# Modulation terms on TensorE, another order of products in the first pass, and other banks, in a two-layer decoder trunk

## The chip, the cores and the metric

The kernel runs on one NeuronCore of a Trainium2 chip. The metric is device time in microseconds of one execution, as the median of several runs. An engine here is one of TensorE (PE; its weight loads are shown apart as PEld), VectorE (DVE), ScalarE (ACT), GpSimd (POOL) and SyncE (SP, which here only issues transfers). Each has its own queue, and works it off in order.

## The reference

Two layers over 256 tokens of width 1024, in float32. Each layer mixes tokens and then runs a gated feed-forward network with a short convolution. Layer 0 mixes by attention in three dilated groups of 16 heads of 64, whose results share one softmax; layer 1 by gated linear attention. Each sub-layer is normalised and then shifted and scaled by terms that come from a vector `c`:

```python
mod = jax.nn.silu(c) @ w_ada[i] + b_ada[i]          # 6 pieces of 1024 per layer
sh1, sc1, g1, sh2, sc2, g2 = [m[:, None, :] for m in jnp.split(mod, 6, axis=-1)]
h = rmsnorm(x, norm_mix[i]) * (1.0 + sc1) + sh1
y = dilated_mixture(h, w_in_a[j], w_out_a[j], rel_bias)   # layer 0
x = x + g1 * y
h = rmsnorm(x, norm_ffn[i]) * (1.0 + sc2) + sh2
x = x + g2 * conv_ffn(h, w_up[i], conv_w[i], conv_b[i], w_down[i])
```

In the dilated mixture, `qkv = h @ w_in` gives queries, keys and values of the three groups; the scores get a bias by distance from `rel_bias`; probabilities times values give the output of a head.

## The kernel before

`x` lies transposed, 8 tiles (`KT`) of 128 features by 256 tokens (`T`). Every large product is made of three: an operand is split into a high part in the fast float32 format and a low part that is the remainder, and `mm3` (lines 172 to 177) issues high x high, high x low and low x high. For a weight matrix, `split` (line 155) loads it into a buffer `raw` (four in turn), ScalarE copies it into `whi` (line 165), VectorE subtracts to get `wlo` (line 169); three buffers of each. For the activations, `normed` (line 253) makes `xr = x * a * r` on VectorE (line 257), `hhi` on ScalarE (line 259) and `hlo` on VectorE (line 260).

The modulation terms come in 48 chunks of 2 x 128 terms (`ada_chunk`, line 129): the chunk's weights are loaded, VectorE makes a dot product over 1024 for each term (line 138) with `c_bc`, which is silu of `c` repeated on all partitions, and ScalarE adds bias and scale (lines 146 and 148). Chunk `kt` of layer 0 gives shift and scale of tile `kt`; the others are made further on, by `next_ada`, wherever the program calls it.

The opening: `c` is loaded as one row and spread by TensorE with `ones_d` (`cb`, line 123), ScalarE makes silu of it (line 124); x is squared, half on VectorE (line 357) and half on ScalarE (line 360); VectorE adds tiles of squares (line 363), TensorE sums over partitions (`ms`, line 187), and ScalarE makes the reciprocal root with Ln and Exp (`rstd_of`). `keep_warm` (line 266) puts matmuls of a constant on TensorE. Three small products give the rows of the biases (line 377), which go through a buffer in DRAM (`rows_d`).

The first pass (lines 381 to 395 and 563 to 572) does the work of head pairs 0 and 1 together: `w0` has, for each of the 8 tiles, 15 blocks of 128 columns: queries and keys of pair 0 in three groups, values of pair 0, queries and keys of pair 1. All accumulate in the 8 banks of PSUM, of 512 columns each. The banks are handed out in three rings: `p` of 2, `s` of 4, `t` of 2. Within a tile the products go block by block, three for each block.

Behind it come the pairs: `queries` (line 534) makes queries and keys of one group of a pair (48 matmuls), `evacuate` (line 488) copies them out, `values` (line 523) makes half of the values, `scores` (line 410) the scores in the four `s` banks, `probabilities` (line 428) adds the bias and takes maxima on VectorE (line 438), exponentials on ScalarE (line 447) and normalised probabilities, `turn` (line 457) transposes those on TensorE through a `t` bank and copies them out (line 464), alternating ScalarE and VectorE, and `outputs` (line 467) multiplies with the values. `load_bias` (line 337) reads a pair's biases with eight transfers. The written order after the first pass is: values of pair 1 (first half), scores of pair 0, values of pair 1 (second half), queries of pair 2, transposes and scores of pair 1, and from there a loop over pairs 2 to 7.

The order on each queue is settled when the program is built: a planner simulates the engines and lays each engine's instructions in a row, following data and `behind(...)`. `behind(i)` keeps what is issued inside it on the engine of `i` behind `i` in that row, and does not touch other engines. Every transfer of weights is issued on SP's queue, in turn with those of the bias rows; `c`, the small vectors and the table go through ScalarE's.

## Time and profile before

| | |
|---|---|
| median of 3 runs | 774.31 us (772.75 to 777.1) |
| profiled execution | 777.02 us, span of its instructions 775.1 us |
| instructions | 15908 |
| TensorE busy | 755.9 us, 98% (weight loads 731.5 us, 94%) |
| VectorE busy | 633.7 us, 82% |
| ScalarE busy | 484.7 us, 63% |
| GpSimd busy | 12.4 us, 2% |
| read from HBM | 184.17 MB, 239 GB/s over the span |
| mean granted clock of TensorE | 0.994 |

In a row of the timeline stand the start in us, the length in us, the engine, the line of the kernel, the operation, `out<-in`, the shapes and the count of instructions merged; in brackets the idle time before it and what ended it. In a row of waits stand who waited on which line, for whom, the total in us, how many times, and the longest. Rows of TensorE overlap, since its matmuls are pipelined: the distance between two starts is the cost of one. A float32 matmul is shown as two instructions.

### The profile page before, as it was taken

Reading aid. Unit: us, or ns where it says so; the run is one execution under the profiler, and the core shown is the slowest. Engines: PE = TensorE matmul, PEld = TensorE weight load, DVE = VectorE, ACT = ScalarE, POOL = GpSimd, SP = SyncE. Lnnn points to the kernel's source line nnn. Section 1 sums busy time; section 2 is a strip of 40 time slices with the busy share of each in tenths; the row PEclk is TensorE's granted clock in tenths of the full one; section 3 lists DMA queues with packets and bytes.
Section 4 is the critical chain, followed back from the end, with each engine's and each line's share of the span. In section 5 each row is a group of like instructions: output and inputs, shape, how many; then the busy total and the mean of one; then the engine's idle time right before and its main releaser. Section 6 shows DMA issues by size and latency. Waiting matters only on the chain.

```text
span 775.1 us, 15908 instructions
## 1 busy us (share of the span) xinstructions
PE 755.9 (98%) x6416; PEld 731.5 (94%) x6416; DVE 633.7 (82%) x1136; ACT 484.7 (63%) x948; POOL 12.4 (2%) x36
## 2 busy tenths in 40 slices
PE   8899899999999999999999999999999999999997
PEld 5899899999999999999999998898999999999997
DVE  6996787779879968999998877797667998899662
ACT  5566564655666668766666556746667776667552
POOL 0000000000000010000000100000010000000000
PEclk9999999999999999999999999999999999999999
DMA  8988687686887847767646985966245665555741
GB/s 344 413 296 315 186 315 242 231 327 198 319 313 257 296 163 261 272 224 270 209 160 213 353 297 180 344 243 235 95 166 188 219 218 187 194 199 205 252 161 55
DMA packets 36199, 186.29 MB, mean 240 GB/s; under 512 B 8412, under 2 KB 10972, under 8 KB 19870
## 3 DMA queue, kind: packets, MB, share of 16 engines
q1 hardware_dynamic: 35744, 184.84, 66.8%
q8 instruction: 50, 0.82, 0.4%
q10 hardware_dynamic: 382, 0.45, 0.2%
q14 instruction: 23, 0.19, 0.1%
HBM read 184.17 MB, written 1.10 MB: 239 GB/s over the span
## 4 chain that ended last, share of the span: by engine, by line
PE 71%; DMA 12%; DVE 11%; ACT 3%; issue 1%; SPq 0%; DVEq 0%; ACTq 0%
PE pab L176 10%; PE pab L175 10%; PE pab L177 10%; DMA raw<-in_wqk 8%; DVE wlo L169 5%; PE pd L175 5%; PE pd L177 5%; PE pd L176 5%; DMA raw<-in_wv 3%; PE pqk L175 3%; PE pqk L176 2%; DVE ada_raw L138 2%; PE pqk L177 2%; PE py L175 2%; PE py L176 2%; PE py L177 2%
## 5 line engine op out<-in xcount | busy, mean ns | idle before, releaser
L169 DVE TENSOR_TENSOR wlo<-raw,whi 128x1024 fp32r<-128x1024 f32 (+3 forms) x274 | 291.8, 1098 | 62.8 <-ACT whi L165 62.1
L165 ACT CAST whi<-raw 128x1024 fp32r<-128x1024 f32 (+3 forms) x274 | 245.8, 945 | 131.9 <-PE pab L176 41.3
L177 PE MATMUL pab<-hhi,wlo 128*128 128x256 f32 x672 | 184.9, 276 | 0.0
L176 PE MATMUL pab<-hlo,whi 128*128 128x256 f32 x672 | 184.8, 277 | 0.0
L175 PE MATMUL pab<-hhi,whi 128*128 128x256 f32 x672 | 183.4, 277 | 0.0
L176 PEld LDWEIGHTS pab<-hlo,whi 128*128 128x128 f32 x672 | 126.1, 188 | 0.2
L177 PEld LDWEIGHTS pab<-hhi,wlo 128*128 128x128 f32 x672 | 126.2, 188 | 0.0
L175 PEld LDWEIGHTS pab<-hhi,whi 128*128 128x128 f32 x672 | 125.2, 188 | 0.1
L175 PE MATMUL pqk<-hhi,whi 128*128 128x256 f32 x440 | 120.8, 286 | 2.6 <-ACT hhi L259 2.6
L177 PE MATMUL pqk<-hhi,wlo 128*128 128x256 f32 x440 | 121.7, 281 | 0.0
L176 PE MATMUL pqk<-hlo,whi 128*128 128x256 f32 x440 | 121.6, 280 | 0.0
L138 DVE CUSTOM_DVE_ANT_0 ada_raw<-ada_raw,c_bc 128x1024 f32<-128x1024 f32 x96 | 113.6, 1222 | 6.6 <-DMA ada_raw<-in_w_ada 6.6
L177 PE MATMUL pd<-ghi,wlo 128*128 128x256 f32 x352 | 97.1, 276 | 0.0
L176 PE MATMUL pd<-glo,whi 128*128 128x256 f32 x352 | 97.1, 276 | 0.0
L175 PE MATMUL pd<-ghi,whi 128*128 128x256 f32 x352 | 96.8, 276 | 0.0
L175 PEld LDWEIGHTS pqk<-hhi,whi 128*128 128x128 f32 x440 | 82.3, 191 | 3.8 <-ACT hhi L259 3.1
L177 PEld LDWEIGHTS pqk<-hhi,wlo 128*128 128x128 f32 x440 | 83.4, 190 | 0.3 <-issue 0.3
L176 PEld LDWEIGHTS pqk<-hlo,whi 128*128 128x128 f32 x440 | 83.5, 190 | 0.1
L176 PEld LDWEIGHTS pd<-glo,whi 128*128 128x128 f32 x352 | 66.1, 188 | 0.0
L177 PEld LDWEIGHTS pd<-ghi,wlo 128*128 128x128 f32 x352 | 66.1, 188 | 0.0
L175 PEld LDWEIGHTS pd<-ghi,whi 128*128 128x128 f32 x352 | 65.9, 188 | 0.0
L734 ACT ACTIVATE r<-pab,small 128x256 f32<-128x256 f32 x86 | 46.6, 558 | 15.6 <-DVE r L737 15.5
(210 smaller groups left out, 1266.4 us busy)
## 6 DMA issues: line engine op xcount, KB each, us to landing
ada_raw<-in_w_ada SPq DMA_DIRECT2D x47, 1024.0 KB, 5.8
raw<-in_w_up SPq DMA_DIRECT2D x42, 1024.0 KB, 4.9
raw<-in_w_down SPq DMA_DIRECT2D x32, 704.0 KB, 5.1
raw<-in_wqk SPq DMA_DIRECT2D x18, 1024.0 KB, 6.6
raw<-in_wv SPq DMA_DIRECT2D x14, 768.0 KB, 4.6
raw<-in_w SPq DMA_DIRECT2D x7, 960.0 KB, 6.5
raw<-in_w_out_a SPq DMA_DIRECT2D x4, 1024.0 KB, 7.2
raw<-in_w_v_b SPq DMA_DIRECT2D x4, 1024.0 KB, 6.4
```

Of the source, the lines that this page charges most:

```text
L138: nc.vector.tensor_tensor_reduce(w, w, c_bc, op0=ALU.mult, op1=ALU.add, scale=1.0, scalar=0.0, accum_out=dot,)
L165: copied[0] = nc.scalar.copy(hi[:, c], raw[:, c])
L169: last_lo[0] = nc.vector.tensor_tensor(lo[:, c], raw[:, c], hi[:, c].bitcast(F32), op=ALU.subtract)
L175: mm(ps, a[0], b[0], start=start, stop=False)
L176: mm(ps, a[0], b[1], start=False, stop=False)
L177: return mm(ps, a[1], b[0], start=False, stop=stop)
L734: nc.scalar.activation(r, u[:, :T], AF.Identity, scale=cw[2], bias=col(C_CB + 44 * l + f))
```

## The change

The opening makes the two terms of chunk (0, 0) on TensorE. Its weights are laid out anew on the host, as 16 blocks of 128 x 128. `c` is loaded a second time as columns (`c_col`, each column twice), with silu in `silu_c`; each block is the stationary operand of a matmul with two columns of `silu_c` moving, and the sums for shift and scale accumulate in one bank, from which ScalarE reads. The other chunks stay on VectorE. `keep_warm(4)` moves ahead of `cb`. Tiles 4 to 7 of the squares are no longer added on VectorE: the mean square takes five matmuls instead of two. `keep_warm(3)` and the rows of the biases go behind the new matmuls.

In the first pass, a tile's products go by part: first high x high for all 15 blocks, then `whi` with `hlo`, then `wlo` with `hhi`. The preparation is written out, with VectorE's order fixed: the tile's dots, `xr`, first half of `wlo`, `hlo`, second half; the next tile's dots behind that. For the first three tiles ScalarE's order is fixed too: the terms, half of the cast, `hhi`, the other half. The banks of pair 0 are `s`, `t`, `t`, its values in `p`, `p`; those of pair 1 `s`, `s`, `s`.

Behind the pass the copies out go groups 1, 2, 0 of pair 0 first, then pair 1. Then come, in this order, the queries and keys of group 0 of pair 2 (in a `t` bank), the scores of pair 0, both halves of the values of pair 1, the scores of pair 1, and the loop. `probabilities` is cut in two (`maxima` and the rest), and pair 1's second part and pair 0's outputs go into the loop's first turn. In `turn`, tiles 2 and 3 take banks of ring `s`, in all pairs.

```diff
--- before.py
+++ after.py
...
     c_row = wspl.tile([P, 2048], F32, tag="whi", name="c_row")
     nc.scalar.dma_start(c_row[:1, :D], I["c"])
+    c_col = const.tile([P, 2 * KT], F32, name="c_col")
+    nc.scalar.dma_start(c_col, I["c_col"])
...
+    def keep_warm(n):
+        ps = bank("warm")
+        for i in range(n):
+            mm(ps[:, :P], ones_d, ones_d, start=True, stop=True)
+    keep_warm(4)
+    silu_c = const.tile([P, 2 * KT], F32, name="silu_c")
+    nc.scalar.activation(silu_c, c_col, AF.Silu)
     c_bc = const.tile([P, D], F32, name="c_bc")
...
+        if (l, n) == (0, 0):
+            ps = bank("mod", "p")
+            for i in range(2 * KT):
+                last_mod[0] = mm(ps[:, 2 * (i % 2) : 2 * (i % 2) + 2], raw[:, P * i : P * i + P], silu_c[:, i // 2 * 2 : i // 2 * 2 + 2],
+                   start=(i == 0), stop=(i == 2 * KT - 1))
...
+            if (l, n) == (0, 0):
+                dot = ps[:, 2 * s : 2 * s + 1]
+            else:
...
-    for n in (0, 4):
-        for m in (2, 1):
-            last_add = nc.vector.tensor_tensor(sq[:, n : n + m, :], sq[:, n : n + m, :], sq[:, n + m : n + 2 * m, :], op=ALU.add)
-        if n == 0:
-            with behind(last_add):
-                last_add = scale_terms(0)
+    for m in (2, 1):
+        last_add = nc.vector.tensor_tensor(sq[:, 0:m, :], sq[:, 0:m, :], sq[:, m : 2 * m, :], op=ALU.add)
+    with behind(last_add):
+        scale_terms(0)
...
-    r = rstd_of([sq[:, 0, :], sq[:, 4, :]])
+    r = rstd_of([sq[:, i, :] for i in (0, 4, 5, 6, 7)])
+    with behind(norm_ops[1]):
+        term = ada_chunk(0, 0, dmas=2)
...
+    with behind(norm_ops[0], last_mod[0]):
...
+    n0 = 15 * P
+    halves0 = (slice(0, n0 // 2), slice(n0 // 2, n0))
+    before_dots, cast = (), ()
...
         if kt:
-            w0.append(split(I["w0"][kt], 15 * P))
-        else:
-            with behind(chain[0][1]):
-                w0.append(split(I["w0"][kt], 15 * P, 2, after=((term,), (chain[0][0],))))
-            with behind(copied[0]):
+            with behind(*before_dots):
+                term = ada_chunk(0, kt, dmas=2 if kt == 1 else 1)
+        a, sh = mod[0, 1, kt], mod[0, 0, kt]
+        xr = tmp.tile([P, T], F32, tag="xr", name="xr")
+        hhi, hlo = h_hi[kt][:, :], h_lo[kt][:, :]
+        last_dve = nc.vector.scalar_tensor_tensor(xr, x[kt], a[:, 0:1], r, op0=ALU.mult, op1=ALU.mult)
+        raw = wraw.tile([P, 2048], F32, tag="raw", name="raw")
+        for c in halves0 if kt < 2 else (slice(0, n0),):
+            last_load[0] = nc.sync.dma_start(raw[:, c], I["w0"][kt][:, c])
+        whi = wspl.tile([P, 2048], F32R, tag="whi", name="whi")
+        wlo = wspl.tile([P, 2048], F32R, tag="wlo", name="wlo")
+        with behind(*((term,) if kt < 3 else ()), *cast):
+            cast = nc.scalar.copy(whi[:, halves0[0]], raw[:, halves0[0]])
+        with behind(*((cast,) if kt < 3 else ())):
+            last_hhi = nc.scalar.activation(hhi, xr, AF.Identity, bias=sh[:, 0:1])
+        with behind(*((last_hhi,) if kt < 3 else ())):
+            cast = (nc.scalar.copy(whi[:, halves0[1]], raw[:, halves0[1]]),)
+        for i in range(3):
+            with behind(last_dve):
+                if i == 1:
+                    last_dve = nc.vector.scalar_tensor_tensor(hlo, xr, sh[:, 0:1], hhi.bitcast(F32), op0=ALU.add, op1=ALU.subtract)
+                    chain[kt] = chain[7] = last_hhi, last_dve
+                else:
+                    c = halves0[i // 2]
+                    last_dve = nc.vector.tensor_tensor(wlo[:, c], raw[:, c], whi[:, c].bitcast(F32), op=ALU.subtract)
+        before_dots = (last_dve,)
+        h.append((h_hi[kt], h_lo[kt]))
+        w0.append((whi, wlo))
+        if kt == 0:
+            with behind(*cast):
...
     def turn(tiles, normed_p, pt):
         for i in tiles:
-            t = bank("t", "t")
+            t = bank("t", "ttss"[i])
...
         if g:
-            last_q[0] = nc.scalar.mul(q[g], pq, 0.125)
-            return nc.vector.tensor_copy(k[g], pk)
+            i = nc.scalar.mul(q[g], pq, 0.125)
+            return i, nc.vector.tensor_copy(k[g], pk)
...
-        return nc.vector.tensor_tensor(kl, pk, kh.bitcast(F32), op=ALU.subtract)
+        nc.scalar.mul(qh, pq, 0.125)
+        i = nc.scalar.copy(kh, pk)
+        nc.vector.scalar_tensor_tensor(ql, pq, 0.125, qh.bitcast(F32), op0=ALU.mult, op1=ALU.subtract)
+        return i, nc.vector.tensor_tensor(kl, pk, kh.bitcast(F32), op=ALU.subtract)
...
-    def values(u, half, pv):
+    def values(u, half, pv, after=(), low=()):
         with behind(*chain[7]):
-            w = split(I["wv"][u - 1, half], 1536)
+            w = split(I["wv"][u - 1, half], 1536, after=(after, after), low=low, late=low)
...
-    def queries(u, g, q, k, tag="p", after=()):
-        w = split(I["wqk"][u - 2, g], 2048, after=(after, after))
+    def queries(u, g, *qk):
+        pq, pk, middle, end = raw_queries(u, g)
+        with behind(evacuate(*qk, g, pq, pk)[1]):
+            next_ada()
+        return middle, end
+    def raw_queries(u, g, tag="p", low=()):
+        w = split(I["wqk"][u - 2, g], 2048, low=low, late=low)
...
-    b0 = [bank("pqk", tg) for tg in "ssspp"]
+    b0 = [bank("pqk", tg) for tg in "sttpp"]
     pqk0 = [b[:, T * i : T * i + T] for b in b0[:3] for i in range(2)]
     pv = b0[3:]
-    b1 = [bank("pqk", tg) for tg in "stt"]
+    b1 = [bank("pqk", tg) for tg in "sss"]
...
     for kt in range(KT):
-        s, e = kt == 0, kt == KT - 1
-        for i in range(2 * NG):
-            mm3(pqk0[i], parts(w0[kt], P * i), h[kt], s and i % 2 == 0, e and i % 2 == 1)
-        wv = parts(w0[kt], 6 * P, NG * P)
-        for t in range(2):
-            ht = [y[:, P * t : P * t + P] for y in h[kt]]
-            mm3(pv[t][:, : NG * P], ht, wv, s, e)
-        for i in range(2 * NG):
-            mm3(pqk1[i], parts(w0[kt], 9 * P + P * i), h[kt], s and i % 2 == 0, e and i % 2 == 1)
+        whi, wlo = w0[kt]
+        hhi, hlo = h[kt]
+        for part, (w, y) in enumerate(((whi, hhi), (whi, hlo), (wlo, hhi))):
+            s, e = part == kt == 0, part == 2 and kt == KT - 1
+            for piece in range(3):
+                if piece == 1:
+                    for t in range(2):
+                        mm(pv[t][:, : NG * P], y[:, P * t : P * t + P], w[:, 6 * P : 9 * P], start=s, stop=e)
+                    continue
+                at, ps = ((0, pqk0), None, (9 * P, pqk1))[piece]
+                for i in ((2, 3, 4, 5, 0, 1), (), range(6))[piece]:
+                    mm(ps[i], w[:, at + P * i : at + P * i + P], y, start=s and i % 2 == 0, stop=e and i % 2 == 1)
...
-    v = by_groups(pv)
-    for qk, pqk, g in ((qk0, pqk0, 0), (qk1, pqk1, 0), (qk0, pqk0, 1), (qk0, pqk0, 2), (qk1, pqk1, 1), (qk1, pqk1, 2)):
-        evacuate(*qk, g, pqk[2 * g], pqk[2 * g + 1])
-    pv = [bank("pv", "p") for _ in range(2)]
-    end = values(1, 0, pv)
+    left = [evacuate(*qk, g, pqk[2 * g], pqk[2 * g + 1])
+            for qk, pqk, g in ((qk0, pqk0, 1), (qk0, pqk0, 2), (qk0, pqk0, 0), (qk1, pqk1, 0), (qk1, pqk1, 1), (qk1, pqk1, 2))]
+    pq, pk, middle, end = raw_queries(2, 0, tag="t", low=left[0][1:])
+    with behind(left[-1][0], left[-3][0]):
+        v0 = by_groups(pv)
     bias = bias_of(0)
     with behind(end):
         s, last = scores(*qk0)
+    qk = new_qk()
+    evacuated = evacuate(*qk, 0, pq, pk)
+    pv = [bank("pv", "p") for _ in range(2)]
     with behind(last):
-        values(1, 1, pv)
-    v0, v = v, by_groups(pv)
-    before = probabilities(s, bias)
-    qk = new_qk()
-    with behind(last):
-        end = queries(2, 0, *qk, tag="t", after=last_q)
-    bias = bias_of(1)
-    with behind(end[1]):
-        turn((0, 1), *before)
+        values(1, 0, pv, low=left[-1][1:])
+    end = values(1, 1, pv, after=left[-1][:1], low=evacuated[1:])
+    with behind(evacuated[1]):
+        next_ada()
+    v = by_groups(pv)
+    before = probabilities(*maxima(s, bias))
+    bias1 = bias_of(1)
+    with behind(end):
         s, last = scores(*qk1)
-    with behind(last):
-        turn((2, 3), *before)
-        outputs(0, v0, before[1])
-    before = probabilities(s, bias)
+    raised = maxima(s, bias1)
...
-            with behind(last):
+        with behind(last):
+            if u > 2:
                 queries(u, 0, *qk)
-        middle, end = queries(u, 1, *qk)
+            middle, end = queries(u, 1, *qk)
...
-        queries(u, 2, *qk)
+        if u == 2:
+            turned_pt, before = before[1], probabilities(*raised)
+        middle, end = queries(u, 2, *qk)
+        if u == 2:
+            with behind(end):
+                outputs(0, v0, turned_pt)
+                turn((0, 1), *before)
         pv = [bank("pv", "p") for _ in range(2)]
         end = values(u, 0, pv)
+        if u == 2:
+            with behind(end):
+                turned = turn((2, 3), *before)
...
     A["w_ada"] = wa.reshape(2, 24, 2, D, P).transpose(0, 1, 4, 2, 3).reshape(2, 24, P, 2 * D)
+    A["w_ada"][0, 0] = wa[0, :2].reshape(2, KT, P, P).transpose(2, 1, 0, 3).reshape(P, 2 * D)
+    A["c_col"] = np.repeat(vec(a["c"]), 2, axis=1)
...
```

38 lines of the change are left out of this document (12 added, 26 removed).

## The prediction

> **What bounds the kernel now.** I read the page first, then TensorE's waits, then the timeline of the first 100 us engine by engine, then busy time by windows.
>
> ```profile
> span 775.1 us, 15908 instructions
> ...
> PE 755.9 (98%) x6416; PEld 731.5 (94%) x6416; DVE 633.7 (82%) x1136; ACT 484.7 (63%) x948; POOL 12.4 (2%) x36
> ...
> PE t L463 <- ACT pt L464: 4.3, 4, 2.6
> ...
> PE pqk L175 <- ACT hhi L259: 2.6, 2, 2.2
> ...
> PE po L471 <- DVE pt L464: 0.9, 1, 0.9
> ...
> PE s L418 <- DVE k L501: 0.8, 1, 0.8
> ```
>
> TensorE is busy for 755.9 of 775.1 us, so no edit can win more than its idle time (19.2 us) plus the time in which it is busy at half clock. The change touches the part up to the attention pairs, where these waits lie. The other waits of the span sum to about 2 us. The reader should see three places.
>
> The first is the opening, up to the first product of the first pass at 13.72.
>
> ```profile
> 3.06 3.74 PE L123 MATMUL cb<-c_row,ones_d 1*128 1x512 f32 x4 [3.06 <-DMA c_row<-in_c]
> 6.74 2.07 PE L270 MATMUL warm<-ones_d 128*128 128x128 f32 x8
> 7.34 1.14 ACT L360 ACTIVATE sq<-x_all 128x512 f32<-128x512 f32 x2
> 8.61 2.33 PE L187 MATMUL ms<-sq,ones_d 128*128 128x256 f32 x4
> 9.58 1.22 DVE L138 CUSTOM_DVE_ANT_0 ada_raw<-ada_raw,c_bc 128x1024 f32<-128x1024 f32 x1
> 10.73 1.21 PE L270 MATMUL warm<-ones_d 128*128 128x128 f32 x6
> 11.80 0.28 ACT L148 ACTIVATE mod<-dot,small 128x1 f32<-128x1 f32 x1
> 11.99 0.38 ACT L146 ACTIVATE mod<-dot,one_b,small 128x1 f32<-128x1 f32 x1
> 12.28 0.97 ACT L165 CAST whi<-raw 128x960 fp32r<-128x960 f32 x1
> 12.41 0.48 DVE L257 SCALAR_TENSOR_TENSOR xr<-x_all,mod,rstd 128x256 f32<-128x256 f32 x1 [0.46 <-ACT mod L146]
> ```
>
> Call T the end of the second modulation term (11.99 + 0.38 = 12.37): all that follows hangs on it. The first product comes 1.35 later, behind one cast and one `hhi`.
>
> The second place is the first pass, eight tiles of x against `w0`.
>
> ```profile
> 13.72 0.50 PE L175 MATMUL pqk<-hhi,whi 128*128 128x256 f32 x2 [0.38 <-ACT hhi L259]
> 21.74 1.01 PE L175 MATMUL pqk<-hhi,whi 128*128 128x256 f32 x3 [2.25 <-ACT hhi L259]
> 49.81 0.34 PE L175 MATMUL pqk<-whi,hhi 128*128 128x384 f32 x1
> 55.02 0.34 PE L175 MATMUL pqk<-whi,hhi 128*128 128x384 f32 x1
> 59.87 0.34 PE L175 MATMUL pv<-whi,hhi 128*128 128x384 f32 x1
> ...
> 31.11 0.48 DVE L257 SCALAR_TENSOR_TENSOR xr<-x_all,mod,rstd 128x256 f32<-128x256 f32 x1
> 31.50 1.22 DVE L138 CUSTOM_DVE_ANT_0 ada_raw<-ada_raw,c_bc 128x1024 f32<-128x1024 f32 x1
> 33.79 0.48 DVE L260 SCALAR_TENSOR_TENSOR hlo<-xr,mod,hhi 128x256 fp32r<-128x256 f32 x1
> 36.33 0.48 DVE L257 SCALAR_TENSOR_TENSOR xr<-x_all,mod,rstd 128x256 f32<-128x256 f32 x1
> 50.21 2.23 DVE L169 TENSOR_TENSOR wlo<-raw,whi 128x960 fp32r<-128x960 f32 x2 [0.27 <-ACT whi L165]
> ```
>
> One tile costs TensorE 55.02 - 49.81 = 5.21 and VectorE 36.33 - 31.11 = 5.22, of which two dots are 2.29 (31.50 to 33.79) and `xr`, `hlo` and two halves of `wlo` 2.93. The two engines are matched. Eight tiles make 41.7 on TensorE, yet the pass takes 59.87 - 13.72 = 46.15. The 4.45 between are the stall of 2.25 at 21.74 and the half clock behind it:
>
> ```profile
> 4.60:8.00 3.40, 3.40 (x9) 1.59 (x8) 2.51 (x5) 1.75 (x4) 0.00 (x0) 1.00 0.99 344
> 8.00:11.40 3.40, 3.35 (x12) 2.45 (x12) 2.86 (x5) 2.18 (x3) 0.00 (x0) 1.00 1.03 396
> 18.20:21.60 3.40, 1.30 (x11) 1.09 (x10) 3.40 (x6) 1.71 (x4) 0.00 (x0) 1.00 1.01 417
> 21.60:25.05 3.45, 3.31 (x13) 3.31 (x14) 3.45 (x7) 2.46 (x5) 0.00 (x0) 0.52 1.01 415
> 79.66:83.07 3.41, 1.14 (x10) 0.93 (x8) 1.37 (x2) 2.42 (x4) 0.00 (x0) 1.00 0.34 55
> 83.07:86.50 3.43, 3.05 (x15) 3.06 (x16) 3.43 (x11) 0.69 (x2) 0.00 (x0) 0.52 0.85 356
> ```
>
> Columns: window, length, busy time of PE, PEld, DVE, ACT, POOL, granted clock, DMA share, GB/s. Twice a window in which TensorE worked for only 1.1 to 1.3 of 3.4 us is followed by one of the same length at clock 0.52. Each costs about 0.48 x 3.4 = 1.65 us over the stall itself.
>
> The third place is the stall at 80.8.
>
> ```profile
> 50.52 0.60 SPq L347 DMA_DIRECT2D bias<-rows_d  x1
> ...
> 66.86 0.63 SPq L159 DMA_DIRECT2D raw<-in_wqk  x1
> 80.62 1.99 ACT L165 CAST whi<-raw 128x1024 fp32r<-128x1024 f32 x2 [3.11 <-DMA raw<-in_wqk]
> 82.64 0.38 ACT L496 ACTIVATE q<-pqk 128x256 fp32r<-128x256 f32 x1
> 83.45 0.90 PE L463 MATMUL t<-ident,pn 128*128 128x128 f32 x3 [2.65 <-ACT pt L464]
> ```
>
> A transpose waits for a bank `t`. That bank is freed by copies on ScalarE, which stand behind casts of weights issued at 66.86 and landed at 80.62. Those weights are not what TensorE needs next: it is ScalarE's queue that is blocked.
>
> **The change, part by part.**
>
> *Opening.* The two dots of chunk (0, 0) leave VectorE (2.3 us from 9.58). TensorE gets 16 matmuls with the weight block stationary and 2 columns moving. A float32 matmul shows as two passes (four copies of the warm matmul make x8), so these are 32. The mean square goes from 2 matmuls to 5, that is from 4 passes to 10, for two pairs of VectorE adds saved. The nearest rows for the new matmul are the cold warm-up (8 passes from 6.74 to 8.61, 0.23 each) and this one, late in the run and with the same 2 columns:
>
> ```profile
> 766.93 0.50 PE L1043 MATMUL ms<-ones_d,sqacc 128*128 128x2 f32 x4
> ```
>
> That is 0.125 a pass. So 32 passes cost 4.0 warm and 7.4 cold. Ten passes of 256 columns cost 4.6 cold (half of a 512-column pass of the 3.06 row, 3.74 / 4 / 2 = 0.46) and 2.3 warm. TensorE is free of `cb` at about 7.0. The operands arrive from then on: the chunk was there by 9.58, the squares at 8.5. The windows put an edge of the clock at 11.4 (25.05 less four times 3.42), where the passes of the 10.73 row begin to cost less. I take the same edge: from 7.0 to 11.4, 4.4 of the 12.0 cold us are done, and the other 7.6 take 3.8, so the terms' sums end at 15.2. Warm throughout it would be 7.0 + 6.3 = 13.3, cold throughout 19.0. The two ScalarE terms take 0.6 more (11.80 to 12.37): T = 15.8, bounds 13.9 and 19.6, against 12.37. So the opening loses 3.4 (1.5 to 7.2). The idle 3.06 before `cb` covers the moved warm-up, whose removal behind `cb` frees nothing on the path. The extra DMA for `c_col` goes before `small`, `tab` and `oh` on ScalarE's queue, and what waits for those, needed only near T, has slack. Chunk (0, 0)'s buffer comes free at 15.2 instead of 11.9, so chunk 2 is asked for 3 us later; its dots come at about T + 9.7, over 10 us after that.
>
> The Trainium skill, TensorE: Matmul & The Clock Gate, section "Part 1: The HAM clock gate", says that the clock doubles once the array was busy through a window of about 3.4 us, whatever the matmuls. By that rule the moved warm-up and `cb`, busy from about 1.2, would run warm before 8. The trace speaks against it for matmuls with one row of weights: TensorE was busy all through 4.60 to 8.00, yet the passes from 8.00 to 11.40 were still at the cold price.
>
> *First pass in order of parts.* TensorE now needs `hlo` a third and `wlo` two thirds into a tile, so the stall of 2.25 goes. VectorE becomes what sets the pace: its order is fixed as dots, `xr`, half of `wlo`, `hlo`, other half, and the next tile's dots stand behind these. The dots no longer run a tile ahead, so each `xr` waits for the terms just made: 0.46, as in the 12.41 row. In the first three tiles the cast also stands behind the term, 0.97 against 0.4 for `xr`: 0.5 more. VectorE: 3.5 for tile 0 (2.93 + 0.5), two tiles of 5.22 + 0.46 + 0.5 = 6.2, five of 5.7; sum 44.4. After the last `wlo` half TensorE has a values piece and a pair piece left, 1.0. The pass ends at T + 45.4, where before it was 59.87 - 12.37 = 47.5: 2.1 won. TensorE's own bound, T + 1.35 + 41.7 and at most 1.65 for a cold start, T + 44.7, lies just under it. With the later T the pass ends 1.3 later than now. Transfers keep up, since the pace of 5.7 asks for less than now.
>
> *Third pair's first weights behind the pass.* VectorE ended its part of the pass at 52.44 (50.21 + 2.23), save one `xr` and `hlo`, 7 us ahead of TensorE, and had the next weights split. Now it ends 1.0 ahead, and must copy a key (0.41) and make half of a `wlo` of 1024 columns (2.36 for two) before the third product: about 0.6 of a new stall. In return the scores come behind 48 matmuls of 0.115 (5.5 us) in place of 24 of 0.17 (4.1), so that their wait of 0.8 goes. On SP's queue the pair's weights now go ahead of the first bias rows, and the loads of the values' weights behind them: eight issues of about 0.6, as in the 50.52 row, 4.8 us. The values are wanted only after the pair's 5.5 us and the scores, so this is hidden behind those; without that cover it would cost up to 4.8.
>
> *The order of pairs and the banks.* The queries of pair 2 leave their bank before the values and scores follow, so the transposes no longer need it at 80.8; tiles 2 and 3 use `s` banks. What is late next is the cast of the weights landed at 80.62, needed only with the second following query step, at about 84. I take the stall (2.65) and its half clock (1.65) as won: 4.3, bounds 0 and 4.3. The other three waits of transposes, 4.3 - 2.65 = 1.7, go too; bounds 0 and 1.7. The 0.9 of `po` I leave.
>
> **Sum.** +3.4 - 2.1 + 0.6 - 0.8 - 4.3 - 1.7 = -4.9. The profiled execution took 777.02 (span 775.1 and 1.9 around it), 2.7 above the median of the runs, 774.31. So 772.1 in such an execution, **769.4** by the median.
>
> **Rivals.**
>
> *TensorE is warm in the opening.* If the moved warm-up and `cb` count, the sums end at 13.3 and T is 13.9: 1.9 less than I took, 767.5. For it: TensorE is occupied from about 1.2. Against it: the two first windows above. (By the Trainium skill's rule on the clock, cited above, this would be the time.)
>
> *The stall moves, so that the gain of the banks is lost.* ScalarE's queue is still an order written before the run. If a cast stands ahead of an evacuation and its transfer is late, the wait and the half clock come back: 769.4 + 4.3 = 773.7. For it: large loads and bias rows still lie close together. Against it: the queue's loads are wanted later in TensorE's order.
>
> *Slower: casts ahead of the terms.* In the pass both casts of a tile may stand on ScalarE between the dot and the second term, as the existing queue does from tile 4 on:
>
> ```profile
> 32.97 1.88 ACT L165 CAST whi<-raw 128x960 fp32r<-128x960 f32 x2
> 34.75 0.38 ACT L146 ACTIVATE mod<-dot,one_b,small 128x1 f32<-128x1 f32 x1
> ```
>
> Today the term has until 36.33; afterwards VectorE, and through it TensorE, waits for it at once. At 1.88 for each of five tiles this is 9.4: 778.8. It makes the kernel slower by over 0.5% from about 1.8 a tile; one cast a tile (4.7) gives 774.1, no change. Against it: the term is ready before the second cast in most tiles.
>
> **Numbers.** Forecast 0.44 (own range 766.5 to 772.5), warm opening 0.24, moved stall 0.20, casts 0.12. A measurement of this kernel can tell about 0.5%, 3.9 us, from no change: faster ends at 770.4, slower begins at 778.2. Faster: the warm opening and about four fifths of the forecast, 0.59. Slower: most of the casts' case, 0.11. Within: 0.30. The range runs from 762 (no loss in the opening, 766.0; the new stall of 0.6 hidden and the 2 us of waits that I left gone, 763.4; a median as far down as the lowest run is now, 1.6) to 777 (one cast a tile, 774.1, and a median as far up as the highest run is now, 2.8).
>
> **What would show it.** Right: the first `xr` near 15.8; 32 passes into the bank of the terms at 0.23 first and 0.125 later; VectorE without a gap over 1 us in the pass and a tile in 5.7; no wait of 2 us for `hhi`; no wait for `t` near 80; clock 1.00 from 25 to 100. Wrong: T at or before 12.4 (then the time is about 766), a tile over 6.5 on VectorE, a wait over 2 us between the pass and the seventh step behind it, or a row of the later pairs with new waits for `s`.

## The result, and the profile after

The changed kernel takes 787.28 us as the median of 6 runs (782.56 to 791.98), beside 774.87 for the kernel before (772.75 to 777.1, 6 runs): a ratio of 1.0159, with an interval of 1.0118 to 1.0200. It is slower by 12.4 us. The forecast was 769.4, with a range that ended at 777. One sentence of the description above is wrong: `keep_warm(4)` does not move ahead of `cb`, a second call of it is added there, and the old one behind `cb` stays.

From the page of the changed kernel, span and busy times:

```profile
span 785.1 us, 16005 instructions
...
PE 767.0 (98%) x6462; PEld 740.4 (94%) x6462; DVE 630.1 (80%) x1130; ACT 484.9 (62%) x949; POOL 12.6 (2%) x36
```

Its waits of TensorE (who waited on which line, for whom, total, times, longest):

```profile
PE pqk L613 <- ACT hhi L409: 5.8, 5, 4.0
PE pv L194 <- DVE k L528: 2.4, 2, 2.0
PE pv L195 <- DVE wlo L188: 1.5, 3, 0.7
```

The waits of transposes for `pt` are gone. In their place stand a wait of the first pass for `hhi` and, late in the loop over the pairs, waits of values for a key copy (2.0 of the 2.4 at 260) and for `wlo`.

The timeline of its opening and first pass (TensorE, VectorE, ScalarE and one issue of SP):

```profile
6.91 2.08 PE L126 MATMUL warm<-ones_d 128*128 128x128 f32 x8
9.63 2.20 PE L148 MATMUL mod<-silu_c,ada_raw 128*128 128x2 f32 x16
11.69 1.97 PE L206 MATMUL ms<-sq,ones_d 128*128 128x256 f32 x8
13.50 1.84 PE L148 MATMUL mod<-silu_c,ada_raw 128*128 128x2 f32 x16
15.92 0.49 DVE L400 SCALAR_TENSOR_TENSOR xr<-x_all,mod,rstd 128x256 f32<-128x256 f32 x1 [7.27 <-ACT mod L165]
...
50.15 0.33 SPq L403 DMA_DIRECT2D raw<-in_w  x1
56.99 1.00 ACT L407 CAST whi<-raw 128x960 fp32r<-128x960 f32 x1 [3.11 <-DMA raw<-in_w]
58.79 0.29 ACT L167 ACTIVATE mod<-dot,small 128x1 f32<-128x1 f32 x1
60.06 1.99 ACT L184 CAST whi<-raw 128x1024 fp32r<-128x1024 f32 x2 [0.98 <-DMA raw<-in_wqk]
61.95 0.38 ACT L165 ACTIVATE mod<-dot,one_b,small 128x1 f32<-128x1 f32 x1
62.37 0.48 DVE L400 SCALAR_TENSOR_TENSOR xr<-x_all,mod,rstd 128x256 f32<-128x256 f32 x1 [4.21 <-ACT mod L165]
63.45 1.65 PE L613 MATMUL pqk<-hhi,whi 128*128 128x256 f32 x6 [3.96 <-ACT hhi L409]
71.04 0.28 PE L194 MATMUL pqk<-hhi,whi 128*128 128x256 f32 x1
71.76 0.38 PE L196 MATMUL pqk<-hhi,wlo 128*128 128x256 f32 x1 [0.32 <-DVE wlo L188]
```

In this execution T is 15.9, the forecast number. The last tile is what goes wrong. Its own casts wait 3.11 for a load that was asked for at 50.15. Its second term then stands on ScalarE behind the two casts of the third pair's first weights, which wait another 0.98 for their load and take 1.99. VectorE waits 4.21, TensorE 3.96, and a stretch at half clock follows (columns as in the windows shown before):

```profile
60.00:64.00 4.00, 0.55 (x2) 0.55 (x3) 1.63 (x3) 2.79 (x4) 0.00 (x0) 0.70 0.53 92
64.00:68.00 4.00, 4.00 (x20) 4.00 (x19) 1.39 (x2) 0.91 (x2) 0.00 (x0) 0.50 0.90 358
```

The first pass ends at 71.04 (the first `pqk` row of line 194) and not at 59.87. The first start of a product, before and after, by tile: `po` (outputs of the heads) 95.4 and 101.4, `py` (the projection behind all pairs) 260.8 and 269.8, `pab` (the feed-forward network) 291.3 and 300.0, `y` (the end) 767.3 and 777.5. So 11.2 are lost by the end of the pass, 5.2 are won back up to `po`, 3.0 of these are lost again in the loop over the pairs, and 10.2 stand at the end of the two profiled executions.

### The profile page after: what moved, and what is told of

It is laid out like the page before. It is cut to its first block, busy times and chain, and to the rows that moved or that the text cites. A ratio compares the mean times of both kernels' runs of the same rounds, so it can differ in the third digit from the quotient of the medians.

```text
span 785.1 us, 16005 instructions
## 1 busy us (share of the span) xinstructions
PE 767.0 (98%) x6462; PEld 740.4 (94%) x6462; DVE 630.1 (80%) x1130; ACT 484.9 (62%) x949; POOL 12.6 (2%) x36
## 4 chain that ended last, share of the span: by engine, by line
PE 67%; DMA 14%; DVE 13%; ACT 3%; issue 2%; SPq 1%; ACTq 0%; DVEq 0%
PE pab L196 10%; PE pab L195 10%; PE pab L194 10%; DMA raw<-in_wqk 7%; DVE wlo L188 6%; PE pd L196 5%; PE pd L194 5%; PE pd L195 5%; DVE ada_raw L157 3%; DMA raw<-in_wv 3%; DMA raw<-in_w 3%; PE py L194 2%; PE py L195 2%; PE py L196 2%; ACT whi L184 2%
## 5 line engine op out<-in xcount | busy, mean ns | idle before, releaser
L188 DVE TENSOR_TENSOR wlo<-raw,whi 128x1024 fp32r<-128x1024 f32 (+2 forms) x258 | 274.4, 1095 | 56.9 <-ACT whi L184 56.2
L184 ACT CAST whi<-raw 128x1024 fp32r<-128x1024 f32 (+2 forms) x258 | 230.9, 942 | 122.3 <-PE pab L195 41.6
L157 DVE CUSTOM_DVE_ANT_0 ada_raw<-ada_raw,c_bc 128x1024 f32<-128x1024 f32 x94 | 111.2, 1223 | 8.2 <-DMA ada_raw<-in_w_ada 8.2
L194 PE MATMUL pqk<-hhi,whi 128*128 128x256 f32 x344 | 97.0, 282 | 0.1
L196 PE MATMUL pqk<-hhi,wlo 128*128 128x256 f32 x344 | 96.0, 279 | 0.3 <-DVE wlo L188 0.3
L195 PE MATMUL pqk<-hlo,whi 128*128 128x256 f32 x344 | 95.7, 278 | 0.0
L196 PEld LDWEIGHTS pqk<-hhi,wlo 128*128 128x128 f32 x344 | 64.8, 188 | 0.9 <-DVE wlo L188 0.5
L194 PEld LDWEIGHTS pqk<-hhi,whi 128*128 128x128 f32 x344 | 64.7, 188 | 0.7 <-issue 0.3
L195 PEld LDWEIGHTS pqk<-hlo,whi 128*128 128x128 f32 x344 | 64.8, 188 | 0.0
L167 ACT ACTIVATE mod<-dot,small 128x1 f32<-128x1 f32 x63 | 18.3, 293 | 61.9 <-DVE dot L157 61.9
```

Of the source, the lines that this page charges most:

```text
L157: nc.vector.tensor_tensor_reduce(w, w, c_bc, op0=ALU.mult, op1=ALU.add, scale=1.0, scalar=0.0, accum_out=dot,)
L167: last = nc.scalar.activation(m, dot, AF.Identity, bias=b)
L184: copied[0] = nc.scalar.copy(hi[:, c], raw[:, c])
L188: last_lo[0] = nc.vector.tensor_tensor(lo[:, c], raw[:, c], hi[:, c].bitcast(F32), op=ALU.subtract)
L194: mm(ps, a[0], b[0], start=start, stop=False)
L195: mm(ps, a[0], b[1], start=False, stop=False)
```

## Experiments

Each kernel was timed beside the kernel before on the same chip, whose median was 774.3 to 775.0 in every set. The changed lines are cuts from the edits: only the lines that matter are shown.

**The opening, undone and alone.** old_opening is the changed kernel with the opening of before (two dots on VectorE, two matmuls for the mean square, warm-up as it was).

```diff
...
-    r = rstd_of([sq[:, i, :] for i in (0, 4, 5, 6, 7)])
+    r = rstd_of([sq[:, 0, :], sq[:, 4, :]])      # and the sums on VectorE, the dots of chunk (0, 0)
...
```

> The changed kernel with the opening of before: the first two terms by dots on VectorE, squares added there, no early warm-up. Theory A (the opening is a plain delay of all that follows): second term at 12.4 instead of 15.9, everything in the pass 3.5 us earlier, the wait for the late cast in the last tile stays at about 4 us; 3 to 4.5 us faster than the changed kernel (783 to 784). Rival D (the pass is paced by transfers, which start at the same time in both): the pass ends at most 1 us earlier and ScalarE waits longer for the weights of w0.

781.7 (1.0091, 1.0058 to 1.0124). The opening costs 5.6 of the 12.4, more than theory A's 3 to 4.5. The wait for `hhi` in the last tile stays, 4.3. opening_alone is the kernel before with only the new opening.

> The kernel before with the new opening alone. Theory A: second term at 15.9 instead of 12.4; TensorE sets the pace in the old pass, so the whole 3.5 us shows, and up to 1.7 more where TensorE begins the pass at half clock: 778 to 780. Rival: VectorE, idle while TensorE makes the terms, and the transfers, which run on, use the time, so that the old stall of 2.25 us at the second tile goes and half of the loss with it: 776 to 777.

785.02 (1.0141, 1.0097 to 1.0184): alone it costs 10.2, more than in its place and more than either theory had. The first `xr` comes at 20.44, and the old order of VectorE then does two tiles' remainders and the dots of the next tiles first, so that the second `xr` comes at 32.77.

**The clock in the opening.** changed_again is the changed kernel unaltered, in a second profile.

> The changed kernel unaltered, a second profile of it. Its first profile shows the clock rise at about 9.6 and the first xr at 15.92; three other kernels with the same opening show no rise before 28 and the first xr at 20.44. Theory M (matmuls with 2 columns do not raise the clock, and an edge at 9.6 is left over by chance from the warm-up): the first xr at either 20.4 or 15.9, the passes of the terms at 0.21 or 0.12 each throughout, and the last xr at 62 to 63 in either case, since the casts that wait for loads set it. Rival N (the first profile is the rule for this kernel): 15.9, and 20.4 belongs to the kernels with moved casts.

The timeline of TensorE in its opening; the run took 789.57:

```profile
9.63 3.41 PE L148 MATMUL mod<-silu_c,ada_raw 128*128 128x2 f32 x16
12.90 3.76 PE L206 MATMUL ms<-sq,ones_d 128*128 128x256 f32 x8
16.46 3.41 PE L148 MATMUL mod<-silu_c,ada_raw 128*128 128x2 f32 x16
```

Its windows there:

```profile
16.00:20.00 4.00, 4.00 (x19) 3.88 (x18) 0.00 (x0) 0.98 (x3) 0.00 (x0) 1.00 0.12 48
24.00:28.00 4.00, 4.00 (x18) 4.00 (x18) 3.15 (x6) 2.27 (x6) 0.00 (x0) 1.00 0.75 260
28.00:32.00 4.00, 4.00 (x34) 4.00 (x34) 4.00 (x6) 1.13 (x2) 0.00 (x0) 1.00 0.80 290
```

Theory M holds on the opening. The passes take 3.41 / 16 = 0.213 by the lengths of the rows (0.204 by the distance of the starts) all through, though TensorE is busy without a gap, and the first `xr` comes at 20.45. In the pass TensorE works off 18 matmuls in the window from 24 to 28 and 34 in the next, so the clock rises near 28. The column of the granted clock says 1.00 in all three windows: here only the price of a pass shows the clock. The same 20.4 stands in one_cast_behind, both_casts_behind and opening_alone: four profiles of five with this opening. The 15.9 was the exception: there the passes turn cheap at about 10.2. Runs of one kernel with this opening can hold either start, so small differences between two such kernels (one alone ranges from 782.56 to 791.98) say little. The last part of the expectation missed: the last `xr` came at 66.00, not at 62 to 63.

wide_terms gives each of the 16 matmuls 128 equal columns in place of 2.

```diff
-  last_mod[0] = mm(ps[:, 2 * (i % 2) : 2 * (i % 2) + 2], raw[:, P * i : P * i + P], silu_c[:, i // 2 * 2 : i // 2 * 2 + 2],
+  last_mod[0] = mm(ps[:, P * (i % 2) : P * (i % 2) + P], raw[:, P * i : P * i + P], silu_c[:, i // 2 * 2 : i // 2 * 2 + 1].to_broadcast([P, P]),
...
```

> The changed kernel with one edit: the 16 matmuls of the first terms move 128 equal columns instead of 2, so that they do the same number of passes and weight loads. Theory W (matmuls with 2 columns do not count as work for the clock): in three of four profiles with the new opening a pass of the terms cost 0.21 and the second term came at 20.4, in one it cost 0.13 and the term came at 15.9. With 128 columns a cold pass costs about 0.23, but the clock rises after some 3 to 5 us of them: the second term comes between 15 and 17.5 every time, TensorE begins the first pass at full clock, and the kernel is 3 to 5 us faster than the changed one (782 to 784). Rival L (weight loads are what costs, the clock is chance): second term at 20.4 or later, no gain or a loss of up to 1.

The same stretch of its timeline:

```profile
9.63 3.55 PE L148 MATMUL mod<-silu_c,ada_raw 128*128 128x128 f32 x16
13.02 1.89 PE L206 MATMUL ms<-sq,ones_d 128*128 128x256 f32 x8
14.74 1.95 PE L148 MATMUL mod<-silu_c,ada_raw 128*128 128x128 f32 x16
```

64 times the columns cost 0.222 a pass in place of 0.213, and the clock is up by 13.0; in all four kernels with wide terms it rose between 9.6 and 13.0. The Trainium skill, TensorE: Matmul & The Clock Gate, section "Part 1: The HAM clock gate", says that a window of about 3.4 us of matmuls raises the clock, whatever they are. The wide terms agree (9.63 to 13.0), the terms with 2 columns do not (cold from 9.63 to past 20, with 8 passes of 256 columns between them). The time is 786.33 (1.0154, 1.0125 to 1.0182), not the 782 to 784 of theory W: the first `xr` comes at 17.27, but the last one at 62.61, since the casts of late loads hold it (62.37 and 66.00 in the two profiles of the changed kernel).

**The late casts.** one_cast_behind holds the cast of the third pair's first weights behind the last `hhi`; both_casts_behind holds the first casts of pair 1's values behind the copies out, too.

```diff
...
-    pq, pk, middle, end = raw_queries(2, 0, tag="t", low=left[0][1:])
+    pq, pk, middle, end = raw_queries(2, 0, tag="t", low=left[0][1:], after=(last_hhi,))
...
-        values(1, 0, pv, low=left[-1][1:])          # second kernel only
+        values(1, 0, pv, after=left[-1][:1], low=left[-1][1:])
```

> The changed kernel with one exchange on ScalarE: the cast of the third pair's first weights goes behind the last tile's second modulation term and hhi. Theory Q (ScalarE's written order before late transfers): the last xr comes at about 58.7 instead of 62.4, the stall of 4.0 us on TensorE and its half clock go, and the pass ends near 65.5 instead of 71.0. But the next cast in the row, that of the values' weights, waits for a load issued at 62.5, and the copies out of the banks stand behind it until 68.7, so TensorE stalls about 3 us again at the third pair's products: 1 to 3 us won in all. Rival D (the transfers set the pace, the order does not matter): the last tile waits as long as before for something else, within 1 us of the changed kernel, and no stall appears behind the pass. Rival S (the stall is all there is): 5 to 6 us won.

> As the kernel before, and the first cast of the values' weights goes behind the copies out of the banks too. Theory Q: the pass ends near 65.5 with no stall behind it of over 1 us, 5 to 6 us faster than the changed kernel, 781 to 782. Rival D: within 1 us of the changed kernel. Either way it stays slower than the kernel before, since the opening (3.5 us) and the longer tile on VectorE remain.

788.66 (1.0174, 1.0130 to 1.0218) and 786.99 (1.0159, 1.0128 to 1.0189): no gain, where theory Q had 1 to 3 and 5 to 6. In the first the stall moves behind the pass, as theory Q had it: TensorE waits 3.3 there for a key copy. In the second the pass itself is mended. From its timeline, VectorE and then TensorE:

```profile
20.44 0.48 DVE L400 SCALAR_TENSOR_TENSOR xr<-x_all,mod,rstd 128x256 f32<-128x256 f32 x1 [11.47 <-ACT mod L165]
39.20 0.49 DVE L400 SCALAR_TENSOR_TENSOR xr<-x_all,mod,rstd 128x256 f32<-128x256 f32 x1 [0.46 <-ACT mod L165]
62.25 0.48 DVE L400 SCALAR_TENSOR_TENSOR xr<-x_all,mod,rstd 128x256 f32<-128x256 f32 x1 [0.46 <-ACT mod L165]
64.12 1.15 DVE L419 TENSOR_TENSOR wlo<-raw,whi 128x960 fp32r<-128x960 f32 x1
...
63.33 0.97 PE L613 MATMUL pqk<-hhi,whi 128*128 128x256 f32 x6
68.72 0.28 PE L194 MATMUL pqk<-hhi,whi 128*128 128x256 f32 x1
82.91 0.44 PE L195 MATMUL pv<-wlo,hhi 128*128 128x384 f32 x1 [1.76 <-DVE wlo L188]
```

From the same T of 20.4 its last `xr` comes 3.75 ahead of that in changed_again (62.25 and 66.00) and the scores of pair 0 start 6.3 ahead (74.8 and 81.1), but `po` only 2.7 (102.5 and 105.2) and `pab` 2.1 (302.2 and 304.3). More than half of what the held cast wins is given back between 75 and 105, where the values now wait (the row at 82.91).

**Both, and then the stall behind them.** wide_terms_casts_behind joins wide_terms and both_casts_behind.

> The changed kernel with both of its edits at once that gained almost nothing one by one: the modulation terms with 128 equal columns moving (median 786.3 alone) and the casts of the third pair's weights held behind the first pass (787.0 alone). Theory 'two delays overlap': the cold opening and the late cast each set a floor of about 62 for the last tile's xr, so only both together move it. First xr near 17.3 as with the wide terms, then three tiles of 6.25 and four of 5.8, last xr at 59.1 (62.25 to 62.6 with each edit alone), no wait for hhi over 1 us, median 783 to 784. Rival 'the opening costs something later': the last xr moves but the time does not, 786 to 787. Rival 'transfers of the first pass set its pace': tiles of 6.2 to the end whatever the opening, last xr at 61 or later, 786.

787.17 (1.0164, 1.0132 to 1.0196): a miss. The last `xr` stays at 61.92, since three tiles now wait for the casts of late loads that stand ahead of their terms, and a new stall follows. Its timeline, VectorE first and then the chain of the stall:

```profile
54.53 0.48 DVE L400 SCALAR_TENSOR_TENSOR xr<-x_all,mod,rstd 128x256 f32<-128x256 f32 x1 [0.46 <-ACT mod L165]
61.92 0.49 DVE L400 SCALAR_TENSOR_TENSOR xr<-x_all,mod,rstd 128x256 f32<-128x256 f32 x1 [2.09 <-ACT mod L165]
...
59.53 1.00 ACT L407 CAST whi<-raw 128x960 fp32r<-128x960 f32 x1 [3.97 <-DMA raw<-in_w]
73.30 0.53 SPq L178 DMA_DIRECT2D raw<-in_wqk  x1
81.46 1.99 ACT L184 CAST whi<-raw 128x1024 fp32r<-128x1024 f32 x2 [6.70 <-DMA raw<-in_wqk]
83.76 0.37 ACT L533 CAST k<-pqk 128x256 fp32r<-128x256 f32 x1
84.83 1.82 DVE L188 TENSOR_TENSOR wlo<-raw,whi 128x768 fp32r<-128x768 f32 x2
85.83 0.69 PE L195 MATMUL pv<-wlo,hhi 128*128 128x384 f32 x1 [4.99 <-DVE wlo L188]
```

The chain reads from top to bottom: weights asked for at 73.30 land at 81.46; their cast stands on ScalarE ahead of the key copy; VectorE's remainder of the values' weights stands behind that copy; TensorE waits 4.99.

terms_before_casts is wide_terms_casts_behind with the casts of a tile behind its term in all eight tiles.

```diff
-        with behind(*((term,) if kt < 3 else ()), *cast):
+        with behind(term, *cast):
```

> As wide_terms_casts_behind (787.2, last xr at 61.92, the intervals of tiles 4, 6 and 8 there 7.07, 6.78 and 7.39), and in tiles 3 to 7 too the casts of a tile stand behind its term on ScalarE. Theory F (a load of the pass is issued only when its buffer is free, lands some 7 later, and holds up the next xr only through the two casts that stand ahead of the term): every tile takes 6.25, last xr at 60.4 or up to 0.5 beside it, first product of the last tile 1.1 behind, end of the pass 5.2 behind that, 66.7 in place of 68.2, median 785 to 786. Rival G (the loads set the pace whatever the order on ScalarE): intervals of 6.8 and more stay, last xr at 61.5 or later, 787.

Its timeline of VectorE, the first and last of eight rows, and a row of its waits of TensorE:

```profile
17.25 0.49 DVE L400 SCALAR_TENSOR_TENSOR xr<-x_all,mod,rstd 128x256 f32<-128x256 f32 x1 [7.62 <-ACT mod L165]
61.01 0.48 DVE L400 SCALAR_TENSOR_TENSOR xr<-x_all,mod,rstd 128x256 f32<-128x256 f32 x1 [0.46 <-ACT mod L165]
```

```profile
PE pv L195 <- DVE wlo L188: 5.1, 2, 4.4
```

Theory F holds for the pass: seven intervals of 6.25. The time is 789.1 (1.0184, 1.0153 to 1.0215), not the expected 785 to 786. The values stall for 4.4 behind the pass, but for 5.0 in wide_terms_casts_behind too, so why this kernel is not faster than that one is not shown. The next kernel puts the casts of the following query step behind the copies out, once with the new opening and once with that of before.

```diff
...
-            middle, end = queries(u, 1, *qk)
+            middle, end = queries(u, 1, *qk, after=evacuated[:1] if u == 2 else ())
```

> As terms_before_casts (789.1; the first pass is regular there, but the values of pair 1 stall for 4.4 on their low part and half a clock follows, 84 to 88 at 0.58), and the casts of the second query step of pair 2 stand on ScalarE behind the copies out of the first. Theory K (what the first pass won was given back by ScalarE's queue: that cast waits 3 to 7 for its load, the key copy stands behind it, the low parts of the values' weights stand behind the key copy on VectorE): no wait of values for a low part over 1 between 75 and 92, clock 1.00 there, and 4.4 + 1.6 less: 782.5 to 784.5. Rival L (the load itself is what is late, for the next step too): the stall moves to the second query step's first product, 786 to 790.

> The same edits (casts of the third pair's weights behind the pass, terms ahead of casts, copies out ahead of the next cast) with the opening of before: all of the change but its opening, with its three late casts moved. First xr at 12.4 and then every 6.25, last xr at 56.1, end of the pass at 62.4. Theory K: 4.9 under copies_before_next_cast, 777.5 to 779.5, which is what the tiles of 6.25 in place of 5.22 cost beside the kernel before. Rival L: 780 or more.

786.82 (1.0146, 1.0116 to 1.0175) and 783.65 (1.0117, 1.0091 to 1.0143). Theory K falls, and the stall moves as rival L had it: no value waits for a low part any more, and the query step waits as long. From the timeline of copies_before_next_cast:

```profile
85.74 1.99 ACT L184 CAST whi<-raw 128x1024 fp32r<-128x1024 f32 x2 [3.78 <-DMA raw<-in_wqk]
88.65 0.26 ACT L545 COPY v<-pv 64x128 f32<-64x128 f32 x1
88.97 0.58 PE L194 MATMUL pqk<-hhi,whi 128*128 128x256 f32 x1 [4.89 <-ACT v L545]
```

It is again a cast that waits for its load with copies out behind it, here those of the values, whose bank the query step needs. The late load itself makes 2.7 of the 4.9 (half of the cast is done only at 86.7), the copies behind it the other 2.2. The opening's price in this pair is 3.2, with a first `xr` at 15.83 and 11.70.

**The rest of the change, without the new opening.** Four kernels build it up, all with the opening of before and both casts held. pairs_order_alone has the new order behind the pass, with two banks for the transposes as before, pairs_order_and_banks also takes `s` banks for tiles 2 and 3, parts_order also the order of parts, old_opening_casts_behind also the new preparation. banks_alone is the kernel before with the banks only.

```diff
-            t = bank("t", "t")
+            t = bank("t", "ttss"[i])
```

> The kernel before (its opening, its first pass and order of products, two t banks) with the new order of pairs behind the pass and the two casts held behind. Theory P (the new order removes the stall of 2.65 near 80, its half clock and the wait of 0.8): 770 to 771, faster than before by 4 to 5. Rival V (VectorE has the third pair's weights to split just when the pass ends, and later pairs get new waits): 773 to 776.

> The same with four banks for the transposes. Theory B1 (the four banks take away the waits for t, 1.7 us, and nothing else): 1 to 2 us faster than the new order alone. Theory B2 (in the changed kernel these waits went, but waits of values for a bank of the pair before and for wlo came, 3.9 us in the later pairs): 1 to 3 us slower than the new order alone.

> As pairs_order_and_banks (776.0: opening and preparation of the first pass as before, new order of pairs, four banks, casts held behind), and the first pass takes the order of parts: the other half of the edit whose preparation went from 776.0 to 779.9. Theory H (the loss of 3.9 is in the preparation: each tile's dots behind the tile before, so that VectorE's interval grows from 5.22 to 5.76 or 6.25 and TensorE has the whole last tile, 5.2, still ahead when the last hhi is made): with the old preparation xr comes every 5.22 to 5.4, end of the pass at 59 to 60.5, median 774 to 776.5. Rival J (the order of parts itself costs, since TensorE then needs both casts of a tile in its first third): waits for hhi or whi of 2 or more, end of the pass past 61, 778 or more.

> The changed kernel with the opening of before, and both late casts on ScalarE (third pair's first weights, first values' weights) behind the work that does not depend on them. Theory Q (the late cast ahead of the last term is worth its stall of 4.3 and the half clock behind it): 4 to 6 us faster than with the old opening alone (781.7), 776 to 778. Rival D (the load of those weights is late anyway, and TensorE waits for it a little later): within 1.5 us of 781.7, with a new wait for wlo or whi at the third pair's first products.

> The kernel before with one edit: tiles 2 and 3 of the transposes take s banks. Theory P (as predicted): the waits of transposes for a copy out (4.3 in all, 2.65 of it at 80.8 with a half-clock window of 1.65 behind it) go, and nothing comes in their place: 771 to 773. Theory Q (what the runs with the new order of pairs showed): the waits for t go, but the values then wait for a p bank held by the key copy on VectorE (pv for k 2 or more, where the kernel before shows under 1), and the time is 774 to 776. Rival: the s banks come too late for the scores, pairs of 2 us for s show, 777 or more.

| kernel | median | ratio and interval |
|---|---|---|
| pairs_order_alone | 778.81 | 1.0057, 1.0031 to 1.0083 |
| pairs_order_and_banks | 776.00 | 1.0016, 1.0001 to 1.0031 |
| parts_order | 777.29 | 1.0032, 1.0004 to 1.0061 |
| old_opening_casts_behind | 779.94 | 1.0058, 1.0028 to 1.0088 |
| banks_alone | 775.94 | 1.0020, 0.9998 to 1.0042 |

The waits of TensorE in pairs_order_alone, in pairs_order_and_banks and in banks_alone:

```profile
PE t L471 <- ACT pt L472: 6.5, 4, 3.3
```

```profile
PE pv L189 <- DVE k L500: 5.2, 4, 2.0
PE pv L190 <- DVE wlo L183: 1.5, 3, 0.6
```

```profile
PE t L463 <- ACT pt L464: 2.6, 1, 2.6
```

The new order alone is slower than both of its theories had it: the transposes wait 6.5, beside 4.3 in the kernel before. The four banks end these waits and win 2.8 there; the waits for a key copy that theory B2 expected stand in their place. On the kernel before the banks win nothing, though not as theory Q has it: a transpose still waits 2.6 for `pt`, and `pv` waits 1.0 for `k`, beside 0.8.

Theory H fits the first pass: with the old preparation `xr` comes every 5.2 to 5.4 again from the second tile on, and the first product behind the pass at 59.76, beside 61.43 in old_opening_casts_behind. The order of parts moves the time by 1.3 and the new preparation by 2.6 more. The intervals of neighbours overlap, so neither is told from nothing alone; the two together, 3.9, are. old_opening_casts_behind lies 1.8 under old_opening, between its theory Q and its rival D.

**A version that might beat both.** keys_first is pairs_order_and_banks with the values' casts and remainders behind the query and key copies that free their banks; keys_first_dots_later also puts a chunk's dots behind those remainders; parts_order_keys_first is keys_first with the order of parts.

```diff
...
-        end = values(u, 0, pv)
+        end = values(u, 0, pv, after=copied_out[1][:1], low=copied_out[1][1:])
...
```

> The new order of pairs with four banks and the opening and first pass of before (776.0, waits of pv for k 5.2 and for wlo 1.5), with one more edit: from pair 2 on the values' casts stand behind the query copy of the step that frees their p bank, and their low parts behind the key copy, so that the copy that frees the bank is never queued behind the remainders of weights that arrive late. Theory R (the waits are made by the order on VectorE's queue): pv for k falls below 1.5 and the time to 771 to 773. Theory S (VectorE has too much to do there, whatever its order): the wait turns up as pv for wlo, 3 or more in all, and the time stays at 775 to 777.

> As keys_first, and the two dots of the chunk that follows the second query step of each pair go behind the remainders of the first half of the values, with their transfer behind that of those weights. Theory R: both waits of values fall below 1 each (6.7 before), 770 to 772. Theory S: the dots are then late or block the next step, and the time is 775 to 777.

> keys_first (773.5) with the order of parts and the old preparation. If both gain where they are, and do not share a wait: theory H gives 772 to 774, with pv for k under 1.5 and the end of the pass at 59 to 60.5; rival J 775.5 or more.

773.53 (0.9986, 0.9965 to 1.0007), 784.47 (1.0142, 1.0105 to 1.0180) and 774.08 (0.9999, 0.9977 to 1.0022). The waits of TensorE in keys_first and in keys_first_dots_later:

```profile
PE pv L189 <- DVE k L500: 0.9, 1, 0.9
```

```profile
PE pv L190 <- DVE wlo L183: 7.5, 4, 1.9
PE pqk L189 <- ACT v L517: 6.1, 4, 2.8
```

In keys_first the wait for `k` falls from 5.2 to 0.9, as theory R has it, and 2.5 are won over pairs_order_and_banks; transposes wait 2.7 again, and beside the kernel before there is no difference that can be told. Moving the dots as well makes new waits, for low parts and for copies of values, and misses both theories. The order of parts adds nothing to keys_first. No version beats the kernel before.

## Why the prediction was wrong

By medians, with 774.7 for the kernel before over all sets, the change adds up like this: new order of pairs with four banks +1.3 (to 776.0), order of parts +1.3, new preparation +2.6, the casts not held +1.8 (779.9 to 781.7), opening +5.6 (to 787.3). Only the opening is told from nothing by itself; the other four are together. The last two depend on their order: with the casts held, the opening costs 7.0 (779.94 to 786.99); with the new opening, holding the casts wins nothing (787.3 to 787.0).

**Opening: forecast +3.4, bounds 1.5 to 7.2; T was 15.9 once and 20.4 four times, +3.5 and +8.0.** The 15.9 that fits the forecast is luck: the terms began 2.6 later than taken, and the clock rose at about 10.2 in place of 11.4 (the first 16 passes took 2.20, the next 16 warm 1.84, and 3.41 is the cold price). Two steps failed. "I take the same edge": the clock edge of the kernel before was carried over to a stretch in which 2-column matmuls had taken the place of 128-column ones, and with these it did not rise in four profiles of five, while it was up by 13.0 in all four with wide ones. And "from 7.0": the terms began at 9.63, since the old warm-up still stood ahead of them (6.91 to 8.99), with two passes of the mean square behind it. The opening with that warm-up really moved was not run. The price of a cold pass, 0.23, was near (0.204 by starts). The upper bound of 19.6 lay 0.8 under what is usual. The rival of a warm opening is refuted: the warm-up and `cb` did not keep the clock up.

**First pass: forecast T + 45.4, measured T + 48.3 without any stall** (68.72 - 20.44 in both_casts_behind), where before it was T + 47.5. The intervals were right, 6.25 and 5.76 for 6.2 and 5.7. What failed is "TensorE has a values piece and a pair piece left, 1.0". TensorE can begin the last tile only with its `hhi`, 1.08 behind `xr` (62.25 to 63.33), and then has the whole tile before it, 5.39 (63.33 to 68.72). VectorE is done at 65.27, so 3.45 are left, not 1.0. Instead of 2.1 won, 0.8 are lost: the stall of 2.25 and its half clock went, but longer intervals on VectorE and a whole last tile behind them cost more.

**"Transfers keep up": wrong.** What counted was when a load could be asked for, not the pace. The last tile's weights are asked for at 50.15, right when VectorE has made the remainder of the tile two before (48.93 to 50.08), whose buffer they take, as `raw` has four in turn; they land 6.8 later. In the kernel before they were asked for at 41.66. That the buffer is the reason is read from these rows and was not tried. This is the mechanism of the slower rival (778.8, chance 0.12), priced there at 1.88 in each of five tiles: here the tiles' own casts delay two terms by 0.8 each, in the sixth and the last tile. In the last tile the casts of the third pair's first weights, which no part of the sum held, add 3.0 (the second term comes at 61.95, where it would follow the first at 59.0). The stretch at half clock over that tile costs 2.2 more (7.59 from 63.45 to 71.04 for 5.39).

In the changed kernel's own profile the pass sums to this: T +3.5, structure +0.8, late tiles +4.65 (`xr` at 62.37 for 15.92 + 41.8), half clock +2.2. That makes 11.15, for the 11.17 between 59.87 and 71.04.

**Behind the pass: forecast 0.6 - 0.8 - 4.3 - 1.7.** The new stall of 0.6 measured 0.32, and no wait of the scores for `k` is left. The stall at 80.8 is gone, and so are the waits of transposes. Up to `po` 5.2 are won, where 0.6 - 0.8 - 4.3 makes 4.5: this part came as forecast. Yet "needed only with the second following query step" held only with the pass ending 11 late. In the kernels with the new preparation and held casts, whose pass ends earlier, it failed: TensorE stalls 1.8 to 5.0 between 82 and 89, mostly behind a cast that waits for its load. That is the mechanism of the moved stall. In the loop the 1.7 were not won: values wait 2.4 for a key copy and 1.5 for low parts. There it is VectorE's queue, as keys_first showed on the kernel with the old opening and pass. That the weights of that query step land late because their buffer is held until the remainder behind the pass is made, and are asked for behind the bias rows, was argued from the order of the rows and not tried.

## What to carry to other kernels

When the order of work lets TensorE start a tile as soon as its first operand is there, the last tile lies whole behind that operand: cost a pass to the end of TensorE's last tile, not to the end of the engine that paces it. On an engine that works in order, ask of each copy that waits for a load what stands behind it; moving one such copy moved the stall to the next more than once here. Here float32 matmuls with 2 columns took about as long as those with 128 at the same clock (0.213 and 0.222 a pass), and did not raise it.

## What was not expected of the hardware

TensorE, busy without a gap from 9.63 to past 20, stayed at the cold price in four profiles of five. Two thirds of that time 2 columns were moving (0.213 a pass), and 8 passes of 256 columns stood between. With 128 columns in the place of the 2 a pass cost 0.222 cold and 0.122 warm (1.95 / 16), and the clock was up by 13.0 in all four profiles. The granted clock of the windows read 1.00 in the cold stretch all the same, while it read 0.50 in the one behind the late tile.
